# Local attention computed in half sequences, with the row scale in the exponential and a packed rotary step

## The chip, the core and the metric

The kernel runs on one core of a Trainium2 chip. The metric is the device time of one execution in microseconds. The kernel before took 1917.75 us (median of three runs, 1916.19 to 1917.99). The profiled execution, to which all durations below belong, took 1917.69 us.

Engines: PE (TensorE) multiplies matrices and transposes, DVE (VectorE) and ACT (ScalarE) do elementwise work and can read the accumulators of PE (PSUM, eight banks of 512 fp32 columns), POOL (GpSimd) does elementwise work on SBUF only, and SP starts the transfers.

## The reference, cut to what matters

Two decoder layers over 512 tokens and 16 meta tokens, 1024 channels. Each layer is a gated feed-forward block (2816 wide), a token mixer, and another feed-forward block, with a norm before and after each. The first layer's mixer is a gated linear attention. After it one key and value set is made (4 heads of 64), and the second layer's mixer, which the change rewrites, is a sliding-window attention of 16 query heads over it:

```python
def swa_mixer(hn, w_q, sinks, w_out, k, v, cos, sin):
    q = (hn @ w_q).reshape(B, L, N_KV_HEADS, GROUP, HEAD_DIM)          # hn = rmsnorm(h, g)
    q = (apply_partial_rope(q, cos, sin) * (HEAD_DIM ** -0.5))         # first 16 of 64 channels
    ...
    s = jnp.einsum('bkgnqd,bknsd->bkgnqs', q_blk, k_band)              # 16 meta + 128 previous + 128 own keys
    mask = jnp.concatenate([ones, (j > i)[None] & (blk > 0), (j <= i)[None]], axis=-1)
    p = sink_softmax(s, mask, sink)      # max over the row and the sink; exp; divide by sum + exp(sink - max)
    o_real = jnp.einsum('bkgnqs,bknsd->bkgnqd', p, v_band)
    return o @ w_out
```

The 512 tokens are four blocks of 128 queries. A query i of a block sees the 16 meta keys, the keys j > i of the previous block (none for the first) and the keys j <= i of its own: 16 + 128 keys in all, so one row of 144 scores holds a query's whole softmax. `rmsnorm(h, g)` is h times a gain of each channel times one factor of each token, 1/sqrt(mean of squares + 1e-6). That factor is called the row factor here.

## The kernel before, in words

Channels lie on partitions, tokens along the free dimension. Big matrix products are three fp32r products each (a split weight by a split operand, `mm3`), and every weight tile is fetched by SP into one of eight `raw` buffers and split in two by ACT (line 227) and DVE (line 228) into one of 32 `pair` slots. The small products of the attention are plain fp32.

One Python program writes the order of PE by hand. Other work (evacuations, softmax, weight splits) is put in between by small generators on a clock of its own (`Flow`): every product adds its planned time, and a generator that yields a number goes on that much later. `yield SCORE`, `SOFT`, `NORM`, `STAGGER` and the lag `LAG` are such plans. DVE, ACT, POOL and SP take their instructions from a scheduler's list, each strictly in its order.

A normed operand (`Operand`) is built without the row factor: the tiles hold h times gain, and the factor, spread over the 128 partitions by a product with ones (`rstd`, `factors`, tensor `R`), is multiplied in where a product is evacuated. So the query products of the mixer wait in `x_first` and in `drain` for that tensor.

The mixer `swa` goes so. (1) The queries are eight units `u` of 128 channels, each two heads `e`. The first four are made by `x_first` in two groups of 256 tokens, the other four by `x_units` in products of 512 columns. (2) `evac` calls `rope` (lines 1033 to 1036): DVE shuffles the partitions and multiplies by the cosine table, POOL multiplies by the sine table and adds. The tables `cr`, `sr` were multiplied by the row factor first (line 1114). All 128 partitions go through this, though only 16 channels of each 64 turn. (3) `soft(u)` makes all four blocks of both heads: for each block two products of 64 rows (the two heads, `sc`), 272 keys wide (previous block, meta, own block; 144 for the first block). ACT copies the 144 meta and own scores (line 1149), and DVE overwrites those with j > i from the previous block's scores by a masked copy of 128 columns (line 1150; for the first block from a tile of -1e30, `neg`). DVE takes the row maxima (1155), folds in the sinks (1156, 1158), ACT does the exponentials with row sums (1160) and that of the sink (1161). DVE adds and inverts (1165, 1166) and scales (1168, 1169; of every second head POOL does it). (4) `core(u)` transposes the probabilities on PE (nine transposes), ACT copies the meta part (1180), DVE copies the rest twice under two masks, own (1189) and previous (1190). Then PE makes the values: per block and head three products in one accumulation, with own values, previous values and meta values. Output columns of the two heads lie on different halves of PE's columns. (5) `split` (411, 412) turns the result into an operand, and `out_proj` multiplies by the output weights in two rounds of four units each: round one starts when `core` 0 to 3 are done (columns of 512), round two when 4 to 7 are (two groups of 256, whose end starts the next norm).

Of the kernel before, what the change touches and what calls it, by code (L numbers as in the profile page):

```python
# [16 lines left out]
P = 128  # L17
D = 1024
# [26 lines left out]
STAGGER = 5.0  # L45
SOFT = 5.0
BEHIND = 2.2
NORM = 3.0
LAG = 3
# [75 lines left out]
def trunk_kernel(ctx: ExitStack, tc, a, out):  # L125
# [36 lines left out]
    def mm(o, lhs, rhs, start=True, stop=True, onto=False):  # L162
        inst = pe.matmul(o, lhs, rhs, start=start, stop=stop, skip_group_check=onto)  # L163
        n = 1
        for d in rhs.shape[1:]:
            n *= d
        flow.clock += n / 2400 if rhs.dtype == F32R else max(n / 600, 0.12)
        return inst
# [183 lines left out]
    def rstd(sq, n, dim, half, name, eng=pool, more=0.0):  # L352
# [7 lines left out]
        yv = sm.tile([P, 4], F32, tag="yv", name=f"yv_{name}")  # L360
# [18 lines left out]
        else:  # L379
# [5 lines left out]
            pool.tensor_tensor(yy, yy, zz, op=ALU.mult)  # L385
        dg = sm.tile([P, 272], F32, tag="dg", name=f"dg_{name}", bufs=2)
# [27 lines left out]
    class Operand:  # L414


        def __init__(self, name, gv, groups, rt=None):
            self.name, self.gv, self.groups, self.tiles = name, gv, groups, [None] * KD
            self.ready = set()
            self.rt = rt  # L420
            self.rjob = [None] * len(groups)
            self.accs = [[] for _ in groups]

        def build(self, gi, k):
# [5 lines left out]
            dve.scalar_tensor_tensor(  # L430
# [9 lines left out]
        def factors(self, gi, eng=pool):  # L440
            if self.rt is None:
# [48 lines left out]
    def x_units(x, nu, groups, evac):  # L490
# [6 lines left out]

        for i in range(nu):
# [6 lines left out]
            for g, p in zip(groups, pst):  # L505
                if all(job.done for job in x.rjob):
# [6 lines left out]
    def x_first(x, nu, evac, opening=False, behind=(), first_ahead=8):  # L513
        behind = list(behind)
        ws = [] if opening else [next_w() for _ in range(nu)]
        set_ahead(8 if opening else 2 * first_ahead)
        jobs = []

        def drain(gi, g, some, pst):
            yield x.rjob[gi]  # L520
# [6 lines left out]
        for gi, some in order + [(1, both)]:  # L527
# [13 lines left out]
            flow.until(lambda: x.rjob[gi] is not None)  # L541
            jobs.append(flow.spawn(drain(gi, g, some, pst)))
            if gi == 0 and some[-1] == nu - 1:
                cap[0] = len(units)
# [14 lines left out]
    def out_steps(hid, groups, split_groups, first, finish=None, tailm=0, packed=False, jobs=()):  # L559
# [60 lines left out]
        for gi, g in enumerate(split_groups):  # L620
            for m in range(KD - tailm, KD):
# [408 lines left out]
    def rope(dst, p, c, s, name):  # L1030
# [4 lines left out]
        pool.tensor_tensor(sh, sh, s, op=ALU.mult)  # L1035
        pool.tensor_tensor(dst, dst, sh, op=ALU.add)


    def shared_kv(x, kp, behind):
        kz = [kp.tile([P, 4, META + P], F32, name=f"kz{j}") for j in range(2)]  # L1040
        vt = flat(pair_tile("vt", F32))[:, :1024].rearrange("p (b v) -> p b v", v=256)
        vmz = [t[:, :512].rearrange("p (c d) -> p c d", d=64) for t in duo("vmz")]
# [18 lines left out]
        def place(drained):  # L1061
# [3 lines left out]
            for j in range(2):  # L1065
# [10 lines left out]
                dve.tensor_copy(vm[:, :P].rearrange("p (c m) -> p c m", m=META), v[:, :META].unsqueeze(1).to_broadcast([P, 8, META]))  # L1076
                yield 1.0
                p = ps(f"vmT{j}")
                transpose(p[:, :P], vm[:, :P])
                for e in range(2):  # L1080
                    dve.tensor_tensor(
                        vmz[j][:, 4 * e : 4 * e + 4],
                        p[:, 64 * e : 64 * e + 64].unsqueeze(1).to_broadcast([P, 4, 64]),
                        rowm[:, 4 * e : 4 * e + 4].unsqueeze(2).to_broadcast([P, 4, 64]),
                        op=ALU.mult,
                    )
                yield 1.0

        job = flow.spawn(place(x_first(x, 4, evac, behind=behind, first_ahead=6)))
        return (kz, vt, vmz), job  # L1090


    def swa(x, kv, finish):
        kz, vt, vmz = kv
        set_ahead(10)
        with tc.tile_pool(name="ap", bufs=1) as ap:
            mgt = ap.tile([P, P], I32, name="mgt")
            sp.dma_start(mgt, a["mgt"])
            mle = ap.tile([P, 2, P], F32, name="mle")
            sp.dma_start(mle, a["mle"])  # L1100
            neg = ap.tile([P, P], F32, name="neg")
            pool.memset(neg, NEG)
            nsink = ap.tile([P, 16], F32, name="nsink")
            dve.tensor_scalar(nsink, vec[:, V_SINK : V_SINK + 16], -1.0, None, op0=ALU.mult)
            cr, sr = duo("csq")
            sp.dma_start(cr, a["cos"])
            sp.dma_start(sr, a["sin"])
            qt = [None] * KD

            def evac(u, g, p):  # L1110
                o, n = g
                if u == 0:
                    for t in (cr, sr):
                        dve.scalar_tensor_tensor(
                            t[:, o : o + n], t[:, o : o + n], 0.125, x.rt[:, o : o + n], op0=ALU.mult, op1=ALU.mult
                        )
                if qt[u] is None:
                    qt[u & ~1], qt[u | 1] = duo(f"q{u}")
                rope(qt[u][:, o : o + n], p[:, :n], cr[:, o : o + n], sr[:, o : o + n], f"q{u}_{o}")

            def score_tile(u, e):
                i = 2 * u + e
                t = flat(Y)[:, i * 576 : (i + 1) * 576] if i < 7 else flat(pair_tile(f"s{u}_{e}", F32))[:, :576]
                return t.rearrange("p (b t) -> p b t", t=144)

            def soft(u, after):
                for jb in after:
                    yield jb
                if u == 1:
                    yield STAGGER  # L1130
                j = u // 4
                qq = qt[u]
                ss = [score_tile(u, e) for e in range(2)]
                nm = sm.tile([P, 2, 4], F32, tag="nm", name=f"nm{u}")
                den = sm.tile([P, 2, 4], F32, tag="den", name=f"den{u}")
                es = sm.tile([P, 2, 4], F32, tag="es", name=f"es{u}")
                mt = sm.tile([P, 8, META], F32, tag="mt", name=f"mt{u}", bufs=3)
                probs[u] = ss, mt

                keys = kz[j].rearrange("p b c -> p (b c)")  # L1140
                for b in range(4):
# [254 lines left out]
```

## Time and profile before

| what | us |
|---|---|
| median of three runs | 1917.75 |
| profiled execution | 1917.69 |
| span of its instructions | 1915.7 |
| PE busy in the span | 1881.8 |
| DVE busy | 1418.3 |
| ACT busy | 1002.1 |
| POOL busy | 219.5 |
| mixer: first query product to first product of the next block (1377.84 to 1547.19) | 169.35 |

The page gives one execution: busy time of each engine, the span in 40 slices, transfers, the chain of work that ended last, and groups of instructions with the idle time in front of them and what ended it. A group's mean is over its shapes unless the view keeps them apart. Times of a timeline row are the start of its first and the length to the end of its last instruction; PE's rows overlap, so differences of starts are used for PE. "DVE w L228" after an arrow is the instruction that was waited for.

### The profile page before, as it was taken

The page shows a single profiled execution, that of the slowest core. Times are in us where ns is not written, and L with a number is a line of the kernel's source. Part 1 is how long each engine was busy: PE and PEld are TensorE (multiplying, and loading weights), DVE is VectorE, ACT ScalarE, POOL GpSimd, SP SyncE. Part 2 cuts the span into 40 slices and gives each one's busy share as a digit, 9 for nine tenths or more (in the row PEclk, how much of TensorE's full clock was granted, in tenths as well). Part 3 has the DMA queues.
Part 4 walks back from the last instruction along what each step waited for, and adds up shares of the span by engine and source line. Part 5 has one row for each costly group of instructions (what it writes and reads, how often), then busy time and mean ns, then how long its engine had stood idle before and what let it go on. Part 6 is the DMA issues. An engine that isn't in the chain of part 4 may idle for free.

```text
span 1915.7 us, 37353 instructions
## 1 busy us (share of the span) xinstructions
PE 1881.8 (98%) x14502; PEld 1797.4 (94%) x14502; DVE 1418.3 (74%) x2868; ACT 1002.1 (52%) x2268; POOL 219.5 (11%) x417
## 2 busy tenths in 40 slices
PE   8999999999999999999999999999988999999997
PEld 8999999999999999999999898989966898989897
DVE  7885858665565788585888786868689679868584
ACT  5663636653246566363674553636546565636363
POOL 2000000321121300000033000000362140000002
PEclk9999999999999999999999999999999999999998
DMA  4332333322113123233341223333320212333331
GB/s 168 97 102 91 104 96 107 114 75 70 56 56 100 56 89 99 92 104 93 112 155 45 72 87 112 97 105 115 109 78 23 78 43 74 98 106 106 104 112 44
DMA packets 102016, 174.61 MB, mean 91 GB/s; under 512 B 11344, under 2 KB 24144, under 8 KB 101840
## 3 DMA queue, kind: packets, MB, share of 16 engines
q1 hardware_dynamic: 101008, 171.59, 28.3%
q8 instruction: 113, 1.85, 0.4%
q10 hardware_dynamic: 832, 0.65, 0.1%
q14 instruction: 63, 0.52, 0.1%
HBM read 170.10 MB, written 2.10 MB: 90 GB/s over the span
## 4 chain that ended last, share of the span: by engine, by line
PE 79%; DVE 14%; ACT 4%; issue 2%; DMA 0%; POOL 0%; SPq 0%; DVEq 0%; ACTq 0%; POOLq 0%
PE y L163 29%; PE a L163 17%; PE x L163 16%; PE c L163 7%; PE d L163 4%; DVE raw L252 2%; ACT w_s L246 2%; DVE w_s L247 2%; DVE w L247 2%; DVE w L228 1%; PE o L163 1%; PE e L163 1%; PE po L163 1%; DVE hidl1f L808 1%; PE ps L163 0%
## 5 line engine op out<-in xcount | busy, mean ns | idle before, releaser
L247 DVE TENSOR_TENSOR w_s<-raw,w_s 128x512 fp32r<-128x512 f32 x288 | 194.1, 691 | 125.0 <-ACT w_s L246 123.0
L163 PE MATMUL y<-hidl0f,w 128*128 128x256 f32 (+1 forms) x2112 | 261.9, 285 | 0.9 <-DVE hidl0f L412 0.6
L163 PEld LDWEIGHTS y<-hidl0f,w 128*128 128x128 f32 x2112 | 259.1, 188 | 1.7 <-DVE hidl0f L412 1.0
L228 DVE TENSOR_TENSOR w<-raw,w 128x512 fp32r<-128x512 f32 x378 | 243.1, 675 | 17.9 <-ACT w L227 16.1
L246 ACT ACTIVATE w_s<-raw 128x512 fp32r<-128x512 f32 x288 | 175.3, 628 | 148.2 <-DVE raw L252 144.5
L163 PE MATMUL y<-hidl1f,w 128*128 128x512 f32 (+1 forms) x1344 | 249.9, 346 | 0.3 <-DVE hidl1f L808 0.2
L163 PEld LDWEIGHTS y<-hidl1f,w 128*128 128x128 f32 x1344 | 212.6, 188 | 33.6 <-DVE hidl1f L808 0.7
L227 ACT ACTIVATE w<-raw 128x512 fp32r<-128x512 f32 x378 | 207.6, 586 | 35.1 <-PE y L163 26.9
L407 POOL TENSOR_TENSOR acc_post<-acc_post,sq_post 128x256 f32<-128x256 f32 (+1 forms) x72 | 59.1, 820 | 1363.1 <-ACT sq_post L406 1362.5
L252 DVE TENSOR_TENSOR raw<-raw,raw 128x512 f32<-128x512 f32 x288 | 198.3, 689 | 5.5
L247 DVE TENSOR_TENSOR w<-raw,w 128x512 fp32r<-128x512 f32 x216 | 148.7, 689 | 40.1 <-ACT w L246 39.2
L246 ACT ACTIVATE w<-raw 128x512 fp32r<-128x512 f32 x216 | 134.0, 621 | 48.1 <-PE y L163 47.8
L163 PE MATMUL x<-x_l0m,w 128*128 128x272 f32 (+1 forms) x1200 | 158.2, 288 | 0.0
L163 PEld LDWEIGHTS x<-x_l0m,w 128*128 128x128 f32 x1200 | 149.3, 189 | 1.1
L589 DVE TENSOR_TENSOR Y<-y,Y 128x256 f32<-128x256 f32 (+2 forms) x176 | 82.5, 474 | 72.2 <-PE y L163 71.7
L163 PE MATMUL a<-zl0f_t,w_s 128*128 128x264 f32 x864 | 117.5, 285 | 0.0
L163 PE MATMUL a<-zl1f_t,w_s 128*128 128x256 f32 x864 | 114.4, 282 | 1.0 <-ACT c L783 0.7
L163 PEld LDWEIGHTS a<-zl0f_t,w_s 128*128 128x128 f32 x864 | 110.3, 188 | 0.2
L163 PEld LDWEIGHTS a<-zl1f_t,w_s 128*128 128x128 f32 x864 | 107.2, 188 | 2.8 <-ACT c L783 2.5
L163 PE MATMUL x<-x_l0f,w 128*128 128x256 f32 (+1 forms) x768 | 100.0, 290 | 6.9 <-ACT w L227 5.9
L163 PEld LDWEIGHTS x<-x_l0f,w 128*128 128x128 f32 x768 | 96.7, 192 | 8.2 <-ACT w L227 5.9
L163 PE MATMUL x<-x_l1f,w 128*128 128x256 f32 (+1 forms) x576 | 92.6, 320 | 0.0
(483 smaller groups left out, 3302.0 us busy)
## 6 DMA issues: line engine op xcount, KB each, us to landing
raw<-in_w_in SPq DMA_DIRECT2D x352, 256.0 KB, 2.9
raw<-in_w_out SPq DMA_DIRECT2D x96, 256.0 KB, 3.3
raw<-in_gla_in SPq DMA_DIRECT2D x50, 256.0 KB, 3.3
raw<-in_w_last SPq DMA_DIRECT2D x48, 256.0 KB, 3.0
raw<-in_w_out SPq DMA_DIRECT2D x64, 128.0 KB, 2.9
raw<-in_gla_out SPq DMA_DIRECT2D x16, 256.0 KB, 2.8
raw<-in_w_q SPq DMA_DIRECT2D x16, 256.0 KB, 3.9
raw<-in_swa_out SPq DMA_DIRECT2D x16, 256.0 KB, 2.7
```

The source lines that it names most:

```text
L163: inst = pe.matmul(o, lhs, rhs, start=start, stop=stop, skip_group_check=onto)
L227: act.activation(w[:, 0, :m], raw[:, :m], AF.Copy)
L228: dve.tensor_tensor(w[:, 1, :m], raw[:, :m], w[:, 0, :m].bitcast(F32), op=ALU.subtract)
L246: act.activation(w[:, 0, :512], src, AF.Copy)
L247: dve.tensor_tensor(w[:, 1, :512], src, w[:, 0, :512].bitcast(F32), op=ALU.subtract)
L252: dve.tensor_tensor(dst, dst, src, op=ALU.add)
L407: pool.tensor_tensor(sums[0][:, :n], sums[0][:, :n], t[:, :n], op=ALU.add)
L589: dve.tensor_tensor(y, p[:, :n], y, op=ALU.add)
L808: dve.scalar_tensor_tensor(t.hid[:, 1, g], t.h, -1.0, t.hid[:, 0, g].bitcast(F32), op0=ALU.mult, op1=ALU.subtract)
```

## The change

- Row factor. `rstd` is cut in two: `root` gives the factors as a [tokens of a block, blocks] column, and also their inverse. Where an operand has a `column` (only the mixer's), `factors` stops there, and nothing waits for the spread tensor. The scores stay without the factor of their query; the exponential takes it as a per-partition `scale`, and the row maximum is multiplied by it.
- Sink. It becomes column 144 of the score row (sink times inverse factor), so it goes through maximum, exponential and sum with the rest. The exponentials of line 1161 and the additions of 1156, 1158 and 1165 become one small product that writes the column and one on the maxima.
- Rotary. `evac` is one ACT copy with scale 1/8. `turn` then gathers the 16 turning rows of each head of four units into one 128-row tile: four products with a selection matrix `sel` (32 columns each). DVE shuffles, multiplies twice and adds, and eight transfers on SP put the rows back (three `turn`s: two of 256 tokens for the first four units, one of 512 for the others). `rope`, which the keys still use, does all on DVE.
- Halves. A visit is one unit and two blocks: 16 visits, in the order units 0 to 3 first half, 0 to 3 second half, then 4 to 7 likewise. Its scores go into four banks, 144 and 128 columns for each block and head, and evacuation takes two blocks at a time (ACT 288, DVE's masked copy 2x128). For the first block the -1e30 scores come from a product of `ones` with `neg`.
- Values. ACT copies all transposed probabilities, DVE only those of the own block under one mask. The products are: all probabilities with the previous block's values, own ones with the difference `dv` of own and previous values, and meta (64 rows now instead of 128). Products of the two heads alternate.
- Order. `pace` starts a visit each `PERIOD`; `LAG` is 5 visits; output round one waits for visits 0 to 7, round two for 8 to 11, and only its second token group for 12 to 15 (`second`). Loading of output weights is held back until the query products are done (`held`, `cap`).

```diff
-STAGGER = 5.0
-SOFT = 5.0
+SOFT = 7.0
 BEHIND = 2.2
-NORM = 3.0
-LAG = 3
+NORM = 5.0
+LAG = 5
+PERIOD = 4.5
+GATHER = 3.0
+TURN = 9.0
+PROBS = 2.5
...
+        if inverse is not None:
+            eng.tensor_tensor(inverse, aa, yy, op=ALU.mult)
+        return yy
+    def rstd(sq, n, dim, half, name, eng=pool, more=0.0):
+        yy = root(sq, n, dim, name, eng)
+        c, nch = yy.shape
...
+            if self.column is not None:
+                o, n = self.groups[gi]
+                yield FACT
+                root(self.accs[gi], n, D, f"{self.name}_{o}", eng, *self.column[gi])
+                yield CHAIN
+                return
...
-        pool.tensor_tensor(sh, sh, s, op=ALU.mult)
-        pool.tensor_tensor(dst, dst, sh, op=ALU.add)
+        dve.tensor_tensor(sh, sh, s, op=ALU.mult)
+        dve.tensor_tensor(dst, dst, sh, op=ALU.add)
...
+                act.activation(qd[u // 2][:, u % 2, o : o + n], p[:, :n], AF.Copy, scale=0.125)
+            def turn(half, g, after_jobs):
+                for jb in after_jobs:
                     yield jb
+                yield GATHER
+                o, n = g
+                pk, sh = (t[:, o : o + n] for t in duo(f"turn{half}_{o}"))
+                p = ps(f"turn{half}_{o}")[:, :n]
+                for u in range(4):
+                    mm(p[32 * u : 32 * u + 32], sel, qd[2 * half + u // 2][:, u % 2, o : o + n], cost=0.2)
+                while (1, KD - 1) not in x.ready:
+                    yield SCORE
+                first = dve.stream_shuffle(sh, p, TURN_SHUFFLE)
+                after(x.built, first)
+                dve.tensor_tensor(pk, p, cr[:, o : o + n], op=ALU.mult)
+                dve.tensor_tensor(sh, sh, sr[:, o : o + n], op=ALU.mult)
+                dve.tensor_tensor(pk, pk, sh, op=ALU.add)
+                for u in range(4):
+                    for e in range(2):
+                        rows = qd[2 * half + u // 2][64 * e : 64 * e + 16, u % 2, o : o + n]
+                        sp.dma_start(rows, pk[32 * u + 16 * e : 32 * u + 16 * e + 16])
+                yield TURN
...
+            visits = [(u, hf) for us in (range(4), range(4, KD)) for hf in range(2) for u in us]
...
+                pa, pb = ([ps(f"s{n}{u}_{hf}{e}") for e in range(2)] for n in "ab")
+                for c in range(2):
+                    b = 2 * hf + c
+                    qs = [qq[rows[e], META + b * P : META + (b + 1) * P] for e in range(2)]
                     for e in range(2):
...
-                        act.activation(s[:, b], p[:, n - 144 : n], AF.Copy)
-                        dve.copy_predicated(s[:, b, META:], mgt, p[:, :P] if b else neg)
+                        mm(pa[e][:, c * 144 : (c + 1) * 144], qs[e], kz[j][rows[e], b], cost=0.1)
+                    for e in range(2):
+                        o = pb[e][:, c * P : (c + 1) * P]
+                        if b:
+                            mm(o, qs[e], kz[j][rows[e], b - 1, META:], cost=0.085)
+                        else:
+                            mm(o, ones[rows[e]], neg[rows[e]], cost=0.085)
+                for e in range(2):
+                    t = s[:, 2 * e : 2 * e + 2]
+                    act.activation(t[:, :, :144], pa[e][:, :288].rearrange("p (c k) -> p c k", k=144), AF.Copy)
+                    dve.copy_predicated(
+                        t[:, :, META:144], mgt.unsqueeze(1).to_broadcast([P, 2, P]),
+                        pb[e][:, : 2 * P].rearrange("p (c k) -> p c k", k=P),
+                    )
+                while x.rjob[hf] is None:
                     yield SCORE
...
+                rc, ri = x.column[hf]
+                pairs = lambda t: t.rearrange("p (e c) -> p e c", c=2)
+                both = lambda t: t.unsqueeze(1).to_broadcast([P, 2, 2])
+                sinks = vec[:, V_SINK + 2 * u : V_SINK + 2 * u + 2].unsqueeze(2).to_broadcast([P, 2, 2])
+                dve.tensor_tensor(pairs(s[:, :, 144]), sinks, both(ri), op=ALU.mult)
+                dve.tensor_reduce(nm, s, axis=AX.X, op=ALU.max, negate=True)
+                dve.tensor_tensor(pairs(nm), pairs(nm), both(rc), op=ALU.mult)
+                for c in range(4):
+                    act.activation(
+                        s[:, c], s[:, c], AF.Exp, scale=rc[:, c % 2 : c % 2 + 1], bias=nm[:, c : c + 1],
+                        accum_out=den[:, c : c + 1],
+                    )
...
+                dve.reciprocal(den, den)
+                rd = den.unsqueeze(2)
+                mt = sm.tile([P, 4, META], F32, tag="mt", name=f"mt{u}_{hf}", bufs=4)
+                dve.tensor_tensor(mt, s[:, :, :META], rd.to_broadcast([P, 4, META]), op=ALU.mult)
+                dve.tensor_tensor(s[:, :, META:144], s[:, :, META:144], rd.to_broadcast([P, 4, P]), op=ALU.mult)
...
+                pm = ps(f"ptm{u}_{hf}")
+                transpose(pm[:64, :P], mt.rearrange("p c m -> p (c m)"))
+                ptm = sm.tile([64, P], F32, tag="ptm", name=f"pm{u}_{hf}", bufs=2)
+                act.activation(ptm, pm[:64, :P], AF.Copy)
...
+                pta, ptc = (pt[:, i, :512].rearrange("p (c k) -> p c k", k=P) for i in range(2))
+                pb = p.rearrange("p (c k) -> p c k", k=P)
+                act.activation(pta, pb, AF.Copy)
+                own = (lambda t: t) if hf else (lambda t: t[:, 1::2])
+                dve.tensor_tensor(own(ptc), own(pb), mle.unsqueeze(1).to_broadcast([P, 4 if hf else 2, P]), op=ALU.mult)
+                yield PROBS
...
+                kvh = [slice((2 * j + e) * 64, (2 * j + e) * 64 + 64) for e in range(2)]
+                for c in range(2):
+                    b = 2 * hf + c
+                    oo = [o[64 * e : 64 * e + 64, c * P : (c + 1) * P] for e in range(2)]
...
+                        mm(oo[e], vt[:, max(b - 1, 0), kvh[e]], pta[:, 2 * e + c], True, False, cost=0.06)
+                    for e in range(2):
                         if b:
...
+                            mm(oo[e], dv[:, b - 1, kvh[e]], ptc[:, 2 * e + c], False, False, cost=0.06)
+                    for e in range(2):
+                        mm(oo[e], vmz[j][:64, 2 * e + c], ptm, False, True, cost=0.06)
...
+                split(so[u], o[:, :256], (META + 256 * hf, 256))
...
+            drained = x_first(x, 4, evac, held=12)
+            set_ahead(16, 8)
+            turns = [flow.spawn(turn(0, g, [drained[gi]])) for gi, g in enumerate(L1)]
+            for i in range(8):
+                attend(i, turns[i // 4], *cores[max(i - LAG, 0) : max(i - LAG + 1, 0)])
+            x_units(x, 4, L1W, lambda i, g, p: evac(4 + i, g, p))
+            cap[0] = len(units)
+            prefetch()
+            turned = flow.spawn(turn(1, L1W[0], []))
+            for i in range(8, 16):
+                attend(i, turned, cores[i - LAG])
...
+            flow.wait(*cores[:8])
             out_proj(so[:4], L1W, L1, True, packed=True)
-            flow.wait(*cores[4:])
+            flow.wait(*cores[8:12])
             set_ahead(16)
             cap[0] = used[0] + 8
-            out_proj(so[4:], L1W, L1, False, finish, KD, True)
+            out_proj(so[4:], L1W, L1, False, finish, KD, True, second=cores[12:])
```

More of the change, by code (lines that the diff above doesn't have):

```diff
@@ L496, in drain @@
             evac(i, g, p)
+        raw = x.column is not None
         for i in range(nu):
@@ L505, in x_units @@
             for g, p in zip(groups, pst):
[L506 removed]
+                if raw or all(job.done for job in x.rjob):
                     evac(i, g, p)
@@ L1304, in trunk_kernel @@
         nxt, fin = into("l1m", 1, 1, True, lambda k: gain(1, 2, k), L1)
+        roots = kp.tile([P, 2, 4], F32, name="roots")
+        nxt.column = [(roots[:, 0, 2 * g : 2 * g + 2], roots[:, 1, 2 * g : 2 * g + 2]) for g in range(2)]
         ffn(x, L1W, fin)
```

199 lines of the change are left out of this document (81 added, 118 removed).

## The prediction

> **What bounds the kernel now.** I read the engines' shares first, then the chain that ended last, then the mixer cut into three stages: A, the first query products; B, attention beside the other query products until the first output product; C, output products up to the next block. The first fence is the chain by engine, the second one row for each stage: length, then busy us (instructions) of PE, PEld, DVE, ACT and POOL, the granted clock, the DMA share and GB/s.
>
> ```profile
> PE 79%; DVE 14%; ACT 4%; issue 2%; DMA 0%; POOL 0%; SPq 0%; DVEq 0%; ACTq 0%; POOLq 0%
> ```
>
> ```profile
> 1377.84:1406.39 28.55, 26.67 (x222) 26.16 (x221) 23.32 (x63) 13.37 (x32) 16.56 (x29) 1.00 0.10 32
> 1406.39:1476.42 70.03, 60.99 (x408) 43.33 (x408) 58.85 (x169) 38.18 (x158) 25.25 (x32) 0.93 0.17 56
> 1476.42:1547.19 70.77, 69.67 (x543) 58.52 (x543) 46.51 (x129) 43.92 (x138) 13.18 (x16) 1.00 0.16 53
> ```
>
> A and C are PE's. In B PE is idle for 9.0 of 70.03 us and runs at a granted clock of 0.93. The longest waits of PE in the mixer (total, times, longest) say for whom: for DVE, which is busy for 58.85 us of B.
>
> ```profile
> PE ptm L175 <- DVE mt L1168: 4.7, 2, 2.7
> PE o L163 <- DVE pt L1189: 1.7, 1, 1.7
> PE sc L163 <- DVE Y L1150: 1.5, 1, 1.5
> PE o L163 <- DVE pt L1190: 1.1, 1, 1.1
> ```
>
> **The change, stage by stage.** The sum is made against the profiled execution, 1917.69 us, 0.06 under the median of the runs (1917.75).
>
> *A.* Near its end DVE and ACT are behind with `x_l1m`, and PE waits (in brackets):
>
> ```profile
> 1403.20 1.22 PE L163 MATMUL x<-x_l1m,w 128*128 128x256 f32 x8 [1.29 <-ACT x_l1m L429]
> 1405.01 0.74 PE L163 MATMUL x<-x_l1m,w 128*128 128x256 f32 x4 [0.59 <-DVE x_l1m L430]
> 1406.39 5.79 PE L163 MATMUL x<-x_l1m,w 128*128 128x512 f32 x24
> 1412.02 0.59 PE L163 MATMUL r_l1m<-dg_l1m,ones 128*128 128x256 f32 x2
> ```
>
> The change takes the spread of the row factor and the rotary steps of the first group out of DVE's list here; ACT gets four copies. I book both waits as gone, and one `r` product of 256 columns (about 0.25, the pitch of the 512-column ones being (1412.02 − 1406.39)/24 = 0.235): 1.29 + 0.59 + 0.25 = −2.1 us. `turn` waits until the last `x_l1m` is built, so it cannot get ahead of those; bounds −2.1 and 0.
>
> *B, first part: PE's.* 96 query products at 0.235 are 22.5 us. Three visits' scores go between them. A visit has per head 2 x (144 + 128) = 544 columns, as have two blocks before:
>
> ```profile
> 1441.50 0.97 PE L163 MATMUL sc<-kz,q 64*128 64x272 f32 x8
> 1442.41 0.50 PE L163 MATMUL x<-x_l1m,w 128*128 128x512 f32 x1
> ```
>
> that is 0.91 us, and with a change of tile shape on both sides 1.1: 3.3 us. The three `turn`s have 4 x 1024 columns in 32-column tiles: 1.7 us (1024 columns at the 0.91/544 of that row) if four column tiles run side by side, 6.8 if one after another; 2.4, near the first, because head halves do run side by side. Sum 28.2 us. The `turn`s' return is eight transfers each on SP. The nearest rows are a small transfer (median us from issue to landing) and the cost of one issue on SP (328 ns):
>
> ```profile
> rowm<-in_rowmask SPq DMA_DIRECT2D x1, 4.0 KB, 1.7
> L1106 SPq DMA_DIRECT2D csq<-in_cos x1: 328/328/328, 1368.1 to 1368.1; - x1
> ```
>
> 8 x 0.33 + 1.7 = 4.3 us after the last rotary step, behind eight raw loads of output weights that stand ahead of them on SP. There are 18 query products (4.2 us) between the first `turn` and the next, and 39 (9 us) from the second `turn` to the first scores: booked as hidden, late by up to 4 us if not.
>
> *B, second part: the attention alone.* After the query products come eight visits with no other product between them, because output round one needs `core` 0 to 7. PE has some 3 us of work in a visit (scores 1.1, five transposes, 10 or 12 value products), DVE more. Its price by the rows of B (mean ns; the first is line 228 over the whole run):
>
> ```profile
> L228 DVE TENSOR_TENSOR w<-raw,w 128x512 fp32r<-128x512 f32 x378 | 243.1, 675 | 17.9 <-ACT w L227 16.1
> ...
> L228 DVE TENSOR_TENSOR w<-raw,w 128x512 fp32r<-128x512 f32 x12 | 11.1, 953 | 0.0
> L1150 DVE COPY_PREDICATED Y<-mgt,sc 128x128 f32<-128x128 int32 x21 | 5.6, 293 | 0.0
> L1189 DVE TENSOR_TENSOR pt<-pt,mle 128x512 f32<-128x512 f32 x8 | 5.5, 686 | 2.1 <-PE pt L175 2.1
> L1155 DVE TENSOR_REDUCE nm<-Y 128x4 f32<-128x576 f32 x7 | 4.9, 740 | 0.0
> L1169 DVE TENSOR_TENSOR Y<-Y,den 128x512 f32<-128x512 f32 x4 | 2.7, 684 | 0.0
> L1156 DVE TENSOR_TENSOR nm<-nm,nsink 128x4 f32<-128x4 f32 x12 | 1.9, 158 | 0.0
> L1166 DVE RECIPROCAL den<-den 128x4 f32<-128x4 f32 x9 | 1.6, 177 | 0.1
> L1034 DVE TENSOR_TENSOR q<-x,csq 128x256 f32<-128x256 f32 x4 | 1.7, 417 | 0.0
> L1168 DVE TENSOR_TENSOR mt<-s,den 128x64 f32<-128x64 f32 x1 | 0.2, 226 | 0.0
> ```
>
> Two masked copies of 2x128 columns are not there: at least 0.293, at most 0.586 each; 0.43, near the 0.417 of the multiplication with 256 columns. Then two small products 2 x 0.158, the maximum 0.74, reciprocal 0.18, `mt` 0.23, scaling 0.68, the own mask 0.42 (first half) or 0.69, and the split 0.42: 3.83 or 4.10 us. Durations overlap where nothing waits:
>
> ```profile
> 1428.74 1.40 DVE L1155 TENSOR_REDUCE nm<-Y 128x4 f32<-128x576 f32 x2
> 1430.07 0.15 DVE L1156 TENSOR_TENSOR nm<-nm,nsink 128x4 f32<-128x4 f32 x1
> 1430.75 1.29 DVE L228 TENSOR_TENSOR w<-raw,w 128x512 fp32r<-128x512 f32 x2
> ```
>
> (two maxima in 1.33 us, 0.075 less than 0.74 each). With nine such overlaps a visit is 3.3 us: the lower bound. ACT has less than DVE:
>
> ```profile
> L1160 ACT ACTIVATE Y<-Y,nm 128x144 f32<-128x144 f32 x28 | 11.2, 402 | 3.2 <-DVE nm L1156 3.2
> L1149 ACT ACTIVATE Y<-sc 128x144 f32<-128x144 f32 x28 | 6.4, 283 | 9.5 <-PE sc L163 9.5
> L411 ACT ACTIVATE so<-o 128x512 fp32r<-128x512 f32 x3 | 1.8, 598 | 5.6 <-PE o L163 5.6
> ```
>
> four exponentials 1.6, two copies of 288 at about 0.41, meta at most 0.28, probabilities 0.60, split 0.38: 3.7 us. Where DVE waits out all four exponentials in every visit, a visit takes 3.97 + 1.6 = 5.6: the upper bound. I take 4.0, nearer the lower end, because five visits are open at once (`LAG`), so other visits' work can stand between. In this stretch eight weight halves for the output are split too: 8 x 0.61 (pitch of the row above) = 4.9; not 0.95 each as in B now, but near the 0.675 of the whole run, as in B POOL runs beside DVE (25.25 us busy) and will have no rotary work any more. 8 x 4.0 + 4.9 = 36.9 us, and B 28.2 + 36.9 = 65.1 instead of 70.03: −4.9 us, bounds −10.5 and +7.9.
>
> *C.* PE sets it; the edits by PE's pitch. Value products now: in PE records, two per product, over C (tile `o`: PE busy 12.56), and in starts:
>
> ```profile
> 1476.42:1547.19 70.77, 12.56 (x177) 10.85 (x176) 3.44 (x5) 2.97 (x5) 1.00 0.16 53
> ```
>
> ```profile
> 1507.74 0.27 PE L163 MATMUL o<-pt,vmz 128*64 128x128 f32 x1
> 1507.85 0.27 PE L163 MATMUL o<-pt,vmz 128*64 128x128 f32 x1
> ```
>
> One record per 0.11 us and head when both halves run. The after kernel has 4 x 10 + 4 x 12 = 88 products, 176 records, alternating: 88 x 0.109 = 9.6, and 0.1 to begin in each of eight visits, 10.4: −2.2. The quoted wait of 1.1 on line 1190 goes: −1.1. Scores of five visits (2720 columns a head) instead of two units (1920): 800 x 0.91/544 = +1.3. Four more `ptm` transposes at about 0.12: +0.5. Against it stand changes of tile shape. The nearest row is one in the gated attention:
>
> ```profile
> 564.48 0.39 PE L163 MATMUL po<-wg,vt 128*128 128x128 f32 x2
> 564.70 0.39 PE L163 MATMUL po<-f,st 128*128 128x128 f32 x2
> 565.02 0.39 PE L163 MATMUL pn<-am,vm 16*128 16x16 f32 x2
> ```
>
> pairs start 0.22 apart, with the change 0.32: 0.10 for one. The meta products now have 64 rows, which makes three more in a visit, and `ptm` 64 columns, one more: 8 x 4 x 0.10 = +3.2 (bounds 0, as if they overlapped, and 8). C: +1.7 us, bounds −3 and +6. The Trainium skill ("TensorEngine Tiling (Array Packing)", Tiling Modes, Key Properties) says that changing the tiling mode, not just the tile, drains the engine. That speaks against this part, and the 0.10 above agrees in sign. By a full drain at each the time would be that of rival (2); without any cost of a change it is 1909.5.
>
> *Shared keys.* `rope` puts POOL's two passes on DVE, which is full there:
>
> ```profile
> 1010.00:1020.00 10.00, 10.00 (x85) 10.00 (x85) 10.00 (x27) 6.74 (x17) 6.82 (x9) 1.00 0.01 2
> ```
>
> but PE is full as well, so mostly hidden: +0.3, from −0.5 (POOL no longer beside DVE) to +3.4 (both passes of two keys at 0.42 and 0.69 exposed, with their products).
>
> Sum: −2.1 − 4.9 + 1.7 + 0.3 = −5.0, 1917.7 − 5.0 = 1912.7 us.
>
> **Rivals.** (1) *Better:* visits at 3.3 us and tile changes that cost nothing: −5.6 − 3.2, 1904. For it: DVE's starts when nothing waits. Against it: a visit crosses PE, ACT and DVE seven times. (2) *Costly tile changes:* a change costs 0.2 instead of 0.10: 32 x 0.1 = +3.2, 1916, no change. For it: the step of 0.10 was seen between pairs, with later weights already loaded. The Trainium skill's rule on drains leads here. (3) *Late rows:* `turn`'s transfers wait behind the raw loads; the first scores come up to 4 us late: 1916, no change. Against it: the nine us before the first scores, and DMA at 0% of the chain. (4) *Slower:* the stretch has no product to fill PE, so any wait in it is time. ACT keeps its order; the next visit's score copies stand behind this visit's exponentials, and these behind DVE's maximum. If the two engines take turns, a visit costs 5.3 (most of the 1.6 us added): +10.4, 1923. From 4.6 us a visit on nothing is gained, from 5.1 it is slower by over 0.2%. For it: ACT's exponentials now wait for DVE (3.2 us in the row above), and PE's longest waits end with DVE. (5) *It does not do what it says:* the visits' products move between output products anyway and C takes back what B gives (+4.9): 1917.6, counted with (2).
>
> **How the numbers follow.** Forecast 0.36 (its own range 1907 to 1915), better 0.17, costly changes and give-back 0.17, late rows 0.07, slower 0.23. A measurement here tells about 0.2% (3.8 us) from no change: faster under 1913.9, slower over 1921.6. The forecast is faster in four fifths of its range (0.29), with better 0.46; the rest of the forecast with (2), (3) and (5) makes 0.31; slower 0.23. The range goes from 1903 (a tenth of the lower cases outside) to 1923, half of the slower case: about 0.15 is left out.
>
> **What would show it.** The first output product should start at about 1469.4 instead of 1476.42, A should have no wait on `x_l1m`, the scores of the first visit should follow the query products with no wait for SP, visits should come 4.0 us apart with DVE over 90% busy, line 228 should fall from 953 to about 680 ns in B, and C should last 72.5 us. The prediction is wrong if the visits come 5 us apart, with ACT and DVE both idle in turn; if score or value products wait more than 0.15 us at each change of shape; or if C grows by more than 5 us.

## The result, and the profile after

The changed kernel takes 1919.76 us (median) against 1917.74 us: a ratio of 1.0013, 95% interval 1.0007 to 1.0019. That is 0.13% slower, inside the 0.2% that I called no change, and not the gain that was forecast. The profiled execution has a span of 1917.7 us, 2.0 more than before.

Stages of the kernel after (length; busy us of PE, PEld, DVE, ACT, POOL with instructions; granted clock; DMA share; GB/s): up to the mixer, A, B, C, the rest.

```profile
0.00:1378.97 1378.97, 1369.86 (x10809) 1336.53 (x10810) 1013.14 (x1997) 719.32 (x1546) 129.93 (x285) 1.00 0.31 96
1378.97:1405.04 26.07, 25.93 (x221) 25.68 (x219) 19.34 (x48) 15.51 (x39) 10.55 (x21) 1.00 0.27 81
1405.04:1475.83 70.79, 64.43 (x514) 45.79 (x514) 43.94 (x119) 43.24 (x140) 2.34 (x12) 0.93 0.12 38
1475.83:1549.65 73.82, 73.26 (x596) 59.57 (x595) 45.33 (x117) 51.84 (x145) 8.81 (x13) 1.00 0.18 58
1549.65:1917.70 368.05, 355.83 (x2527) 332.66 (x2525) 275.88 (x524) 186.54 (x395) 27.26 (x50) 0.99 0.29 89
```

| stage | before | forecast | after |
|---|---|---|---|
| up to the mixer | 1377.84 | +0.3 | +1.13 |
| A | 28.55 | −2.1 | −2.48 |
| B | 70.03 | −4.9 | +0.76 |
| C | 70.77 | +1.7 | +3.05 |
| rest | 368.51 | 0 | −0.46 |
| sum | | −5.0 | +2.0 |

In B, DVE's work fell from 58.85 to 43.94 us, and the stage did not get shorter. B in two parts: query products with the first scores, then, from the first transposition to the first output product, the eight visits alone ("the stretch").

```profile
1405.04:1433.98 28.94, 28.94 (x170) 21.25 (x170) 9.27 (x28) 10.41 (x30) 2.34 (x12) 1.00 0.04 10
1433.98:1443.41 9.43, 6.62 (x63) 4.64 (x63) 9.36 (x23) 8.65 (x24) 0.00 (x0) 0.96 0.34 104
1443.41:1449.73 6.32, 6.26 (x41) 4.10 (x42) 5.06 (x15) 3.75 (x14) 0.00 (x0) 0.53 0.67 218
...
1466.65:1469.96 3.31, 3.31 (x24) 2.77 (x22) 1.18 (x3) 2.62 (x10) 0.00 (x0) 0.51 0.02 5
```

The first part is 28.94 us, as worked out (28.2). The stretch is 1475.83 − 1433.98 = 41.85 us instead of 36.9. In it PE waits for 6.3 us in all, and for two pieces, 6.32 and 3.31 us, its clock is granted at about half. The waits of PE in the mixer:

```profile
PE o L166 <- DVE pt L1250: 3.1, 4, 1.2
PE o L166 <- ACT pt L1248: 2.9, 2, 1.6
PE sa L166 <- ACT Y L1202: 0.6, 1, 0.6
PE sb L166 <- DVE Y L1203: 0.2, 1, 0.2
```

In the lines of the kernel after, L1202 is ACT's copy of the scores, L1203 the masked copy, L1216 and L1217 the maximum and its factor, L1219 the exponential, L1224 the reciprocal, L1227 and L1228 the scaling, L1248 and L1250 the two copies of the transposed probabilities, L422 and L423 the split, L231 and L230 a weight half (on DVE and on ACT); L166 stands for all products and L178 for all transpositions. The waits look small and spread. A piece of the chain in order of time shows what they have in common:

```profile
1453.17 2.08 ACT Y L1219 x8
1455.27 0.19 DVE den L1224
...
1455.63 0.78 DVE Y L1203 x2
...
1456.78 0.60 DVE Y L1228
1457.38 0.67 DVE nm L1216
...
1458.81 1.83 ACT Y L1219 x7
...
1460.88 1.97 ACT s L1219 x8
1462.88 0.19 DVE den L1224
```

ACT's exponentials, then DVE, then ACT's exponentials again: the two engines take turns. What could fill DVE's wait is there: the scores of visit 6 are the four rows of PE that begin at 1452.25 and end with the first line below, and ACT's list has them behind the exponentials of visit 5 (the second line is the first of the four), so that they are copied at 1455.15, 1.7 us after they were made, and masked at 1455.63.

```profile
1453.07 0.39 PE L166 MATMUL sb<-kz,q 64*128 64x128 f32 x4
```
```profile
1453.17 0.51 ACT L1219 ACTIVATE Y<-Y,nm,roots 128x145 f32<-128x145 f32 x1
...
1455.15 0.68 ACT L1202 ACTIVATE Y<-sa 128x288 f32<-128x288 f32 x2
```

Waits of DVE and (the three longest) of ACT in the stretch, 6.4 us for DVE in all:

```profile
DVE den L1224 <- ACT s L1219: 2.1, 2, 1.3
DVE pt L1250 <- ACT pt L1248: 1.4, 2, 0.9
DVE den L1224 <- ACT Y L1219: 1.1, 2, 0.8
DVE Y L1203 <- ACT Y L1202: 1.0, 1, 1.0
DVE so L423 <- ACT so L422: 0.8, 2, 0.7
```
```profile
ACT so L422 <- PE o L166: 3.3, 2, 2.4
ACT Y L1219 <- DVE nm L1217: 2.6, 3, 1.3
ACT pt L1248 <- PE pt L178: 1.2, 3, 0.6
```

### The profile page after: what moved, and what is told of

It is laid out like the page before. It is cut to its first block, busy times and chain, and to the rows that moved or that the text cites. A ratio compares the mean times of both kernels' runs of the same rounds, so it can differ in the third digit from the quotient of the medians.

```text
span 1917.7 us, 37635 instructions
## 1 busy us (share of the span) xinstructions
PE 1889.3 (99%) x14658; PEld 1800.2 (94%) x14658; DVE 1397.6 (73%) x2803; ACT 1016.4 (53%) x2262; POOL 178.9 (9%) x379
## 4 chain that ended last, share of the span: by engine, by line
PE 86%; DVE 9%; ACT 3%; issue 2%; DMA 1%; POOL 0%; SPq 0%; DVEq 0%; ACTq 0%
PE y L166 30%; PE x L166 18%; PE a L166 18%; PE c L166 8%; PE d L166 4%; DVE raw L255 2%; ACT w_s L249 1%; DVE w_s L250 1%; DVE w L250 1%; PE o L166 1%; PE e L166 1%; DVE w L231 1%; PE po L166 1%; PE ps L166 0%; DVE hidl1f L834 0%
## 5 line engine op out<-in xcount | busy, mean ns | idle before, releaser
L166 PE MATMUL y<-hidl0f,w 128*128 128x256 f32 (+1 forms) x2112 | 261.9, 285 | 0.9 <-DVE hidl0f L423 0.6
L166 PEld LDWEIGHTS y<-hidl0f,w 128*128 128x128 f32 x2112 | 259.1, 188 | 1.6 <-DVE hidl0f L423 1.0
L231 DVE TENSOR_TENSOR w<-raw,w 128x512 fp32r<-128x512 f32 x378 | 236.3, 655 | 21.0 <-ACT w L230 19.0
L166 PE MATMUL y<-hidl1f,w 128*128 128x512 f32 (+1 forms) x1344 | 251.0, 346 | 0.3 <-DVE hidl1f L834 0.2
L166 PEld LDWEIGHTS y<-hidl1f,w 128*128 128x128 f32 x1344 | 212.3, 188 | 35.2 <-DVE hidl1f L834 1.5
L230 ACT ACTIVATE w<-raw 128x512 fp32r<-128x512 f32 x378 | 207.4, 586 | 41.1 <-PE y L166 30.4
L250 DVE TENSOR_TENSOR w<-raw,w 128x512 fp32r<-128x512 f32 x216 | 148.2, 687 | 29.9 <-ACT w L249 29.2
L166 PE MATMUL x<-x_l0m,w 128*128 128x272 f32 (+1 forms) x1200 | 158.2, 288 | 0.0
L166 PEld LDWEIGHTS x<-x_l0m,w 128*128 128x128 f32 x1200 | 149.3, 189 | 1.1
L166 PE MATMUL a<-zl0f_t,w_s 128*128 128x264 f32 x864 | 117.5, 285 | 0.0
L166 PE MATMUL a<-zl1f_t,w_s 128*128 128x256 f32 x864 | 114.4, 281 | 0.9 <-ACT c L809 0.6
L166 PEld LDWEIGHTS a<-zl0f_t,w_s 128*128 128x128 f32 x864 | 110.3, 188 | 0.2
L166 PEld LDWEIGHTS a<-zl1f_t,w_s 128*128 128x128 f32 x864 | 107.2, 188 | 2.8 <-ACT c L809 2.4
L166 PE MATMUL x<-x_l0f,w 128*128 128x256 f32 (+1 forms) x768 | 100.5, 291 | 6.5 <-ACT w L230 5.9
L166 PEld LDWEIGHTS x<-x_l0f,w 128*128 128x128 f32 x768 | 97.1, 193 | 7.8 <-ACT w L230 5.9
L166 PE MATMUL x<-x_l1f,w 128*128 128x256 f32 (+1 forms) x576 | 92.6, 320 | 0.0
```

The lines of the kernel that those rows point to most:

```text
L230: act.activation(w[:, 0, :m], raw[:, :m], AF.Copy)
L231: dve.tensor_tensor(w[:, 1, :m], raw[:, :m], w[:, 0, :m].bitcast(F32), op=ALU.subtract)
L250: dve.tensor_tensor(w[:, 1, :512], src, w[:, 0, :512].bitcast(F32), op=ALU.subtract)
```

## The experiments

The theories: P, PE's own work with its changes of tile shape holds the stretch; W or D, the amount of work on DVE and ACT holds it; Q, one late copy on ACT; F, PE has no other products there to fill its waits; S, rival (4), an order on ACT makes the engines take turns. All ratios are to the kernel before on the same chip (after itself: 1.0013); the lengths are of one profiled execution each. How far a length varies can be seen at rope_pool: its attention is that of after, and its stretch is 1.4 us longer, at a granted clock of 0.80 against 0.88. So differences of the stretch under 1.4 us tell nothing by themselves.

| run | ratio, 95% | B | stretch, PE's waits in it | C |
|---|---|---|---|---|
| after | 1.0013 (1.0007 to 1.0019) | 70.79 | 41.85, 6.3 | 73.82 |
| uniform_meta | 0.9985 (0.9976 to 0.9995) | 70.16 | 41.21, 7.5 | 70.73 |
| early_halves | 1.0012 (1.0003 to 1.0022) | 71.78 | 41.02, 6.9 | 73.07 |
| early | 1.0059 (1.0044 to 1.0074) | 76.71 | 50.22, 11.8 | 76.98 |
| rope_pool | 1.0013 (1.0004 to 1.0023) | 72.15 | 43.26, 5.2 | 73.61 |
| spread6t | 1.0053 (1.0037 to 1.0070) | 70.18 | another order | 83.04 |
| copy_dve | 1.0015 (1.0005 to 1.0024) | 71.31 | 42.36, 7.3 | 73.57 |
| no_scale | 1.0006 (0.9996 to 1.0015) | 70.17 | 41.39, 5.0 | 73.37 |
| before_alternate | 1.0000 (0.9990 to 1.0009) | 69.88 | none | 70.39 |
| copies_first | 0.9974 (0.9965 to 0.9984) | 65.38 | 36.60, 3.5 | 72.27 |
| copies_first_u | 0.9947 (0.9932 to 0.9962) | 64.50 | 35.72, 5.6 | 68.85 |
| cf_u_eh | 0.9928 (0.9913 to 0.9943) | 61.47 | 32.69, 3.8 | 68.60 |
| cf_early | 0.9935 (0.9918 to 0.9951) | 59.96 | 32.09, 3.0 | 68.57 |

**uniform_meta.**

```diff
-transpose(pm[:64, :P], mt.rearrange("p c m -> p (c m)"))
+transpose(pm[:, :P], mt.rearrange("p c m -> p (c m)"))      # mt padded with zeros to 128 columns
...
-mm(oo[e], vmz[j][:64, 2 * e + c], ptm, False, True, cost=0.06)
+mm(oo[e], vmz[j][:, 2 * e + c], ptm, False, True, cost=0.06)
```

> Meta products and their transposition get the full 128 rows again (rows 64 to 127 of the meta values are zero), so that a visit's value products all have one tile shape; nothing else changes. Theory P (PE's own work, with four changes of tile shape in a visit at about 0.15 us, holds the attention stretch): the output stage C falls by 8 x 0.5 = 4 us from 73.8, the stretch of eight visits by 4 us from 41.9, the kernel goes from 1919.8 to about 1912. Theory W (the stretch is held by waits for DVE and ACT and the clock that falls after them): C falls by 4, the stretch by nothing, since PE waits longer instead; about 1916.

C fell by 3.1, the stretch by 0.6, and PE's waits there grew by 1.2; its granted clock over the stretch was 0.83 instead of 0.88. That is W's pattern: tile shape is a price in C, where PE is the bound, and none that can be told in the stretch. The price, in starts of one visit's value products, after first, then this run (four records are one product of each head):

```profile
1510.53 0.44 PE L166 MATMUL o<-pt,vt 128*64 128x128 f32 x4
1510.80 0.39 PE L166 MATMUL o<-pt,dv 128*64 128x128 f32 x4
1511.12 0.43 PE L166 MATMUL o<-pm,vmz 64*64 64x128 f32 x4
1511.48 0.44 PE L166 MATMUL o<-pt,vt 128*64 128x128 f32 x4
```
```profile
1508.36 0.44 PE L166 MATMUL o<-pt,vt 128*64 128x128 f32 x4
1508.63 0.39 PE L166 MATMUL o<-pt,dv 128*64 128x128 f32 x4
1508.85 0.39 PE L166 MATMUL o<-pm,vmz 128*64 128x128 f32 x4
1509.07 0.39 PE L166 MATMUL o<-pt,vt 128*64 128x128 f32 x4
```

The first step of a group is 0.27 us in both. Then the steps without a change of shape are 0.22 us; with one, 0.32 and 0.36. Over C the value groups of the eight visits take 15.21 us after and 11.65 here, both with PE's waits in them (0.6 and 1.0 us): 3.56/24 changes = 0.15 us each. The undisturbed visits say the same: 1.69 us after and 1.24 here, 0.45 for three changes.

**early_halves.**

```diff
-set_ahead(16, 8)
+set_ahead(16, 12)
+cap[0] = len(units)
+prefetch()
```

> The eight halves of output weights that are split inside the attention stretch are split before it, beside the query products, where DVE is busy for 9 of 29 us. Theory P: only the waits go that stand right behind those halves (1.37 and 0.75 us), 1917 to 1918. Theory W: the stretch falls by the 4.9 us of DVE and by part of the slow clock (4.6 us lost), to about 35; the kernel at 1912 to 1914.

No gain. All eight halves left the stretch, and DVE's busy time in it fell by 4.7 us, ACT's by 3.8; it shortened by 0.8, and the part before it, which took them, grew by 1.8 (30.76). DVE's waits in it grew from 6.4 to 10.2 us instead. So the amount of work does not hold the stretch in this order, and W, as I had put it, falls.

**early.**

```diff
-GATHER = 3.0
-TURN = 9.0
+GATHER = 1.5
+TURN = 6.0
```

> The plan for the turning step is shortened (GATHER 3 to 1.5, TURN 9 to 6), so that the first scores come 12 query products earlier and one whole visit with its values lies between query products instead of behind them. Theory P: the same products in another order, so 0 to -1 us. Theory W: more work of PE stands beside the first visits' waits, the stretch loses 3 to 5 us net; 1915 to 1917. If the turned rows are not there in time, a wait of PE for SP appears ahead of the first scores, up to 3 us, and nothing is gained.

Slower, against every theory. No wait for SP came. In this order of PE, visits 1 and 2 have their values right behind their transpositions, with the next scores behind both, and PE meets the copied probabilities with nothing in between:

```profile
1447.63 0.44 PE L166 MATMUL o<-pt,vt 128*64 128x128 f32 x4 [3.91 <-ACT pt L1248]
```

**rope_pool.**

```diff
-dve.tensor_tensor(sh, sh, s, op=ALU.mult)
-dve.tensor_tensor(dst, dst, sh, op=ALU.add)
+pool.tensor_tensor(sh, sh, s, op=ALU.mult)
+pool.tensor_tensor(dst, dst, sh, op=ALU.add)
```

> For the keys alone, the two rotary passes go back from DVE to POOL. Both theories: the attention is unchanged; the first query product, which starts at 1378.97 instead of 1377.84, comes back by about 1.1 us if those passes are what delays the key stage, and by nothing if it is the other new work there (the difference of values).

The first query product starts at 1378.95, as in after (1378.97): nothing here says that the keys' rotary passes delay it. But it starts at 1378.43 in before_alternate, whose code is that of before up to there (1377.84), and at 1378.8 to 1380.3 in the others; so one execution cannot tell 1.13 us well, about half of them is within what the kernel before varies by, and the cause of the rest is open.

**spread6t.**

```diff
-TURN = 9.0
+TURN = 13.0
...
 mm3(p[:, : g[1]], w, k, x.tiles[k], g, k == 0, k == KD - 1)
+if raw:
+    flow.clock += 0.6
+    flow.pump()
```

> The plan charges each query product of the last four units more time, and TURN goes from 9 to 13 so that the first scores keep some 30 query products ahead of them; so nine of those products come between the transpositions and the values of each of visits 0 to 2, where before all of them stood ahead of visit 0. The work is the same. Theory F (the stretch is long because PE, with nothing else to do, waits in order for each visit's copied probabilities, and its clock falls after those waits): waits in the stretch fall from 6.3 to 2 to 4 us, the slow clock's 4.6 us by half, B from 70.8 to about 66, the kernel 1914 to 1916. Theory D (DVE and ACT have too much to do for eight visits, wherever PE's products stand): B stays within 1 us.

B moved by −0.6 only, and C got worse by 9.2. Yet F is right for the visits that got filler: PE waits 0.5 us in visits 0 to 2 (2.8 in after). In visit 3 it waits 1.6 us; the values of these four end at 1449.5 us, though the mixer began 1.1 later, against 1455.1 in after. Visits 4 to 7, for which no query product is left, then take 26.8 us instead of 20.7. Their largest wait stands where the last `turn` and the weight halves meet on DVE's list:

```profile
1457.48 0.69 PE L166 MATMUL o<-pt,dv 128*64 128x128 f32 x4 [3.12 <-DVE pt L1253]
```

The filler was moved, not added, and the loop that needs it stayed as long as it was. In C the second half's visits come late, which I did not follow further.

**copy_dve.**

```diff
-act.activation(pta, pb, AF.Copy)
+dve.tensor_copy(pta, pb)
```

> The copy of all transposed probabilities goes from ACT to DVE. Theory Q (that copy is late because it stands behind up to eight exponentials in ACT's list): PE's wait for ACT there (2.9 us in two) vanishes, the stretch loses 2 to 3 us, 1917. Theory D (too much work): DVE has 0.69 us more in each visit, the stretch grows by up to 5 us, 1922 to 1925.

```profile
PE o L166 <- DVE pt L1248: 5.5, 4, 2.9
```

That is PE's wait for this copy over the mixer. The wait changed its name, and the stretch stayed (+0.5): the copy is late on either engine. Q falls, and D's 5 us did not come.

**no_scale.**

```diff
-s[:, c], s[:, c], AF.Exp, scale=rc[:, c % 2 : c % 2 + 1], bias=nm[:, c : c + 1],
+s[:, c], s[:, c], AF.Exp, bias=nm[:, c : c + 1],
```

> The exponential without its per-partition scale (the row factor is left out of the scores there, so the probabilities are others; the rest is the same). It prices the scale: one exponential starts 0.49 us after the other, before the change 0.40. If the scale costs that, the pitch comes back to 0.40, ACT has 0.36 us less in a visit, and the stretch loses 0 (filled waits) to 3 us; if it is the 145th column or the accumulation, the pitch stays at 0.49.

Exponentials of after in B, then of this run:

```profile
L1219 ACT ACTIVATE Y<-Y,nm,roots 128x145 f32<-128x145 f32 x28 | 13.9, 498 | 4.5 <-DVE nm L1217 4.5
```
```profile
L1219 ACT ACTIVATE Y<-Y,nm 128x145 f32<-128x145 f32 x28 | 11.3, 406 | 4.3 <-DVE nm L1217 2.9 <-DVE den L1224 1.3
```

It is the per-partition scale that costs 92 ns an instruction, not the 145th column. The stretch lost 0.5 us, the whole kernel nothing that can be told.

**before_alternate.** In the kernel before, the order of the value products alone:

```diff
-for e in range(2):          # a head: own, previous, meta
-    ...
+for e in range(2):
+    mm(oo[e], vt[:, b, kvh[e]], pts[e][0][:, b], True, False)
+for e in range(2):
+    if b:
+        mm(oo[e], vt[:, b - 1, kvh[e]], pts[e][1][:, b - 1], False, False)
+for e in range(2):
+    mm(oo[e], vmz[j][:, 4 * e + b], ptm, False, True)
```

> The kernel before, with the value products of its two heads issued alternately instead of three of one and three of the other; nothing else. A unit's 22 products take 2.8 us from first to last there now. If the halves were out of step, 22 x 0.109 + 0.1 = 2.5 us, 0.3 less in each of eight units, of which the four in C count: C from 70.8 to 69.6, the kernel 1915.5 to 1916.7. If they run side by side anyway: no change.

C fell by 0.4, the kernel by nothing that can be told. By starts, from a unit's first value product to what follows its last, two of the four units in C went from 2.83 and 2.82 us to 2.55 each, the 0.3 us of heads out of step. The other two, where PE waits for DVE's copies (1.1 us before, 1.7 here), went from 7.66 to 7.82. So alternating gives some 0.3 us a unit where nothing waits, 1.1 for four at most, and not the −2.2 that I booked in C.

**copies_first.** A visit's exponentials are issued by the next visit, with an order edge behind that visit's score copies.

```diff
+    moved = act.activation(t[:, :, :144], pa[e][:, :288].rearrange("p (c k) -> p c k", k=144), AF.Copy)
...
+if i and not exped[i - 1].done:
+    for e in exps[i - 1]():
+        after(moved, e)
+    exped[i - 1].finish(flow)
...
-for c in range(4):
-    act.activation(s[:, c], s[:, c], AF.Exp, ...)
-yield SOFT
+exps[i] = exp                # the same four instructions
+yield exped[i]
+yield HELD                   # 2.5
```

> One order is turned round, on ACT alone: the four exponentials of a visit stand behind the score copies of the next visit, not ahead of them; PE's order in the stretch is the same. Theory S (rival 4 of the prediction: DVE and ACT take turns, because the next copies stand behind exponentials that wait for DVE's maximum, 5.2 to 5.6 us a visit): a visit falls to PE's own 3.9 us, waits of PE from 6.3 to under 2, no slow clock, the stretch from 41.9 to 33 to 36, the kernel at 1911 to 1914. Theory D (too much work on DVE and ACT in any order): the stretch keeps 40 to 42 us.

Near S's figures: the kernel takes 1913.77 us, and the stretch goes from 41.85 to 36.60 with the same order of PE in it; PE's waits, 3.5 us, did not fall under 2. DVE's waits in it, 6.4 us in after, are now

```profile
DVE den L1239 <- ACT s L1227: 0.3, 1, 0.3
DVE so L424 <- ACT so L423: 0.3, 1, 0.3
```

and DVE is busy for 35.19 of 36.60 us:

```profile
1434.13:1470.73 36.60, 33.07 (x348) 22.69 (x344) 35.19 (x95) 34.10 (x117) 0.00 (x0) 0.91 0.22 66
```

So a visit fell not to PE's 3.9 us but to what DVE has to do. B is 65.38 us, against the 65.1 of the prediction. One slow piece stays (a granted clock of 0.53 from 1439 to 1445 us), where DVE has the weight halves. The work is the same, and D's 40 to 42 us are excluded. But more than ACT's list moved: the plan's delay before the reciprocal went from `SOFT` to `HELD` after the next visit's exponentials, and DVE's list changed with it (each visit's reciprocal now follows the next visit's maximum, where after has two maxima in a row, at 1457.30 and 1459.63, and then two reciprocals). What is shown is that the order on these two engines held the stretch; ACT's part was not run apart from DVE's.

**copies_first_u** (with uniform_meta's edit) and **cf_u_eh** (and early_halves' edit).

> The same together with 128 rows for the meta products (one tile shape in the values). Under S, PE's own time is now the bound of the stretch, so the 0.4 us a visit that hardly showed there before (0.6 us in all) should show: 3 us less in the stretch and 3 in C than copies_first, 1905 to 1908. Under D: C alone, 3 us less.

> The two edits before and the eight weight halves split ahead of the stretch. Under S, with PE the bound, the halves cost only what they add to waits: 0 to 2 us less than copies_first_u, though in the stretch as it was they cost nothing to measure. Under D: up to 5 us less.

copies_first_u takes 1908.85 us, a little over the 1908 of S. The uniform shape is worth 3.4 in C, but only 0.9 in the stretch, so there PE was still not the bound, as S had it; DVE was, busy for 34.54 of 35.72 us. Hence the weight halves now count: taking them out shortens the stretch by 3.0 us (S: 0 to 2, D: up to 5), where the same edit gave 0.8 as long as the engines took turns. With the order turned, D's account is thus the better one. cf_u_eh is faster than the kernel before: 1904.91 us against 1918.75 (0.9928).

**cf_early** (cf_u_eh with early's two constants).

> The three edits of cf_u_eh with the shorter plan of the run early (GATHER 1.5, TURN 6), which alone cost 9.5 us. Here the scores of a later visit stand between the transpositions and the values of every visit; in early they stood behind the values in visits 1 and 2. If early was slow because the turned rows or the first visits came too soon, this is slower than cf_u_eh by 3 us or more; if it was slow because nothing covered the copied probabilities there, this is within 2 us of cf_u_eh (1903 to 1907).

1904.12 us, as cf_u_eh. So the earlier start need not cost anything; that early paid for the order that came with it fits this, but is not shown, since three other edits stand between the two runs and which of them mends it is not separated.

## Why the prediction was wrong

The range held the time; the direction did not hold, and the 7.0 us between −5.0 and +2.0 sit in these steps.

- **B, the price of a visit (+5.0 of +5.7 in B).** The step that failed: "I take 4.0, nearer the lower end, because five visits are open at once (`LAG`), so other visits' work can stand between." Open visits are no help when their next instruction stands behind a waiting one on the same engine. A visit took 41.02/8 = 5.1 us without any weight halves (early_halves), the last `turn`'s work in it, with DVE and ACT waiting in turn: the sign of being wrong that the prediction had named. Rival (4), given 0.23, named the mechanism, copies behind exponentials behind the maximum, and nearly its price (5.3). Its total of 1923 was too high, because it added the halves' 4.9 us, which in fact filled DVE's waits. With the order on ACT, and DVE's with it, turned round, the stretch fell to 36.60 and B to 65.38.
- **The count of DVE's work came out near, in part by luck.** The sum put the stretch at 36.9, and copies_first has 36.60. But the third `turn` falls into the stretch, and its four DVE passes, 2.4 us by their starts, were not booked there. Without them and the halves (4.8) some 29.4 us are left, 3.7 a visit and not 4.0: the two errors cancel. The masked copy was right (0.43; 0.44 measured). On ACT an exponential was put at 0.40 us, but has 0.49 with its per-partition scale. That is a miss of mine: the Trainium skill ("ScalarE: Activation LUTs", What ACT_TABLE_LOAD costs) says that each per-partition pointer operand adds about 93 ns; this case's 92 ns agrees.
- **C (+1.35).** Values were booked at −2.2 − 1.1 + 2.4 = −0.9; their groups went from 13.30 to 15.21 us, +1.9. Two sizes were off. A change of shape cost 0.15 instead of 0.10 us, +3.56 for +2.4 (rival 2 had 0.2). And without these changes, in uniform_meta, the groups still take 11.65 us, −1.65 for the −3.3 of alternating and the wait: alternating gives 0.3 a unit where nothing waits, and PE still waits for copies there, 0.6 us in after. Scores (+0.83 for +1.3) and transpositions (−0.15 for +1.3 with their change of shape) gave part of it back; output products and their waits took +0.46. The drain that the Trainium skill ("TensorEngine Tiling (Array Packing)", Tiling Modes, Key Properties) names for a change of tiling mode fits the 0.15.
- **A (−2.48 for −2.1):** both waits went, as said.
- **Late rows (rival 3):** the transfers landed 1.8 us after issue (2.1 for the last `turn`; medians), and PE never waited for them.
- **Shared keys (+1.13 for +0.3):** rope_pool gives no sign of the rotary passes; half of it may be variation, the rest is open.
- **Line 228 (now 231)** fell to 681 ns in B, as forecast, and DVE's busy time there fell by 14.9 us. In the order of this kernel the stretch did not follow it.

## What to carry to other kernels

Before costing a loop over two engines by the busier one, write out both lists in order, and look for an instruction that is ready but stands behind one that waits for the other engine; the sum of both is the price until that order is turned. An amount of work that seems free to take away (the halves: 0.8 us) may be worth much more once the order is mended (3.0 us), so a null result on such a chain does not settle that work's cost. Where PE sets the time, one tile shape within a run of small products can pay for padding with zeros (here 3.1 us in C).

## What the runs showed of the hardware

- A per-partition scale in an activation adds 92 ns (498 against 406 for 128x145, after and no_scale).
- A change of tile shape, 128x64 to 64x64 or back, between fp32 products of 128 columns costs about 0.15 us of PE (24 changes, 3.56 us, after and uniform_meta).
- PE's granted clock fell to about half for 6.3 and 3.3 us in the stretch of the kernel after, behind single waits of at most 1.6 us (2.8 us in all in the 6.5 us before the first, 2.2 in the 4.4 before the second). The Trainium skill ("TensorE: Matmul & The Clock Gate", What's actually happening) puts the fall at a whole idle window of some 3.4 us; here no wait was that long.
